# First mixer of a hybrid encoder: a third buffer for queries, keys and gates, all input projections ahead of the second group's values, and one output norm for two heads

## The chip, the cores and the metric

The kernel runs on one core of a Trainium2 chip. The metric is the device time of one execution in microseconds; a profiled execution also leaves a trace, whose span (first to last instruction) is a little shorter than the execution's time. Five engines work side by side: PE (TensorE, matmuls into PSUM), DVE (VectorE), ACT (ScalarE), POOL (GpSimd) and SP, which here only issues DMAs. Each takes its instructions in the order in which the program gives them and waits on semaphores for the others.

## The reference, cut to what matters

The model is four pre-norm residual layers (an even mixer, a feed-forward layer, an odd mixer, a feed-forward layer) over 512 positions of width 1024 in float32. The change is in the even mixer, the first layer:

```python
p = jnp.einsum('bsd,de->bse', h, w_in)
gq, gk, gv, gr, glf, glb, hq, hzf, hzb, hi, hg = _split(p, EVEN_COLS)
a = gla_mixer(gq, gk, gv, gr, glf, glb, wa2, ba, gla_g)          # 4 heads
bm = hgrn2_mixer(hq, hzf, hzb, hi, hg, lb_f, lb_b, hgrn_g)       # 4 heads
y = jnp.concatenate([a, bm], axis=-1)
return jnp.einsum('bse,ed->bsd', y, w_out)
...
# in both: o = bidir_scan(q, k_f, k_b, v, log_gates...); o = head_rmsnorm(o, norm_g); return o * silu(gate)
```

Each head has 64 key and 128 value channels. A gated linear attention runs over the positions in both directions; its output is normalised per head and position, multiplied by a gain and by a gate.

## The kernel before, in words

Heads go in pairs p = 0 to 3: pairs 0 and 1 are the first head group (GLA), pairs 2 and 3 the second (HGRN2). Heads are u = 2p and 2p + 1. A projection matmul multiplies a float32 weight chunk, split into a high and a low part (`h_`, `l_`, made by ACT and DVE in `load_split`), with the input, split likewise (`xh_m`, `xl_m`): 24 matmuls of 512 columns for each tile of 128 outputs.

For a pair the kernel makes queries `q`, keys `k` and gates `a` (tiles for both directions). Then `scores(p)` builds the attention scores: `products(0)`, the diagonal, and then seven levels h = 1, 2, 4, ... 64. At each level PE makes one set of small products in `sc` (two PSUM banks used in turns), DVE multiplies `q` and `k` by the running gate products, and a predicated copy takes the level's products from `sc` into `s`. The last level, 64, goes from `sc` into the score tile `A` on ACT. So PE and DVE take turns, and the next level's products wait for DVE. `attend(p)` follows: transposes of k (`kT`), states (`dS` on PE, `Si` on DVE), outputs `o` in PSUM, the norm of the outputs (Square on ACT, a sum on DVE, a power of -0.5 on POOL in `rstd`, a multiplication on DVE), transposes `oT`, and `finish(u)`, which multiplies with the gate `r` and splits the result into `yh` and `yl` for the output projection `wo`. For heads 4 to 7, `yh` and `yl` take over the buffers of the input tiles `xh_m`, `xl_m` (tag `xh`, `xl`, eight each). The tiles `o` have two buffers.

The order on PE is made when the program is written, by `Sched`. *Jobs* (projections `j_q`, `j_k`, `j_hq`, `j_hz`, values `j_v`, gates `j_gate`, output projection `j_out`) stand in one list and hand PE three matmuls at a time. *Chains* (`gates`, `scores`, `attend`) are put in between: each `yield W[...]` says after how much further matmul work, by an estimate in ns, the chain goes on. `self.sch.now` is that estimate's clock. A `yield` of a condition waits until another chain has got to a point. Nothing in this is decided on the chip; a chain that comes too early there makes PE wait.

The jobs' order before is values of group 0 (`v0`), gates g0 and g1, values of group 1 (`v1`), projections of pair 2 (`h2`: `p_hq2`, `p_hz0`, `p_hz1`), g2, g3, `h3`, g4 to g7, then `wo`. The tiles q, k and a have two buffers, so the projections of pair 2 wait until `attend(0)` has read those of pair 0.

Of the kernel before, what the change touches and what calls it, by code (L numbers as in the profile page):

```python
# [18 lines left out]
S = 512  # L19
# [5 lines left out]
S5PAD = 48  # L25

W = {
# [12 lines left out]
}  # L40

FAST = ("q1", "q2", "qk1", "qk2")
# [93 lines left out]
class Net:  # L136
# [261 lines left out]
    def even(self):  # L398
# [58 lines left out]

        def pair(p):
            if p not in P:
                P[p] = [pool.tile([128, w], F32, tag=n, name=f"{n}{p}", bufs=2)  # L460
                        for pool, n, w in ((ep, "q", S2), (ep, "k", KW), (em, "a", AW))]
            return P[p]

# [65 lines left out]
        def gates(p):  # L529
            af = pair(p)[2]  # L530
            a = dirs(af)
            yield W["z"]
            for d in range(2):
                i = 2 * p + d
                pz = hd_ps([128, S], f"z{i}")
                self.mm(pz, wa[:, i, :], lr)

                b = ba[:, i : i + 1]
                t = et([128, S], "e", f"e{i}", 2)
                nc.scalar.activation(t, pz, AF.Abs, bias=b)  # L540
                V.tensor_scalar(
                    out=a[:, d], in0=pz, scalar1=b, scalar2=0.0, op0=ALU.add, op1=ALU.min)
                nc.scalar.activation(t, t, AF.Exp, scale=-1.0)
                nc.scalar.activation(t, t, AF.Ln, bias=1.0)
                V.tensor_tensor(out=a[:, d], in0=a[:, d], in1=t, op=ALU.subtract)
            nc.scalar.activation(af[:, 0:S2], af[:, 0:S2], AF.Exp, scale=1.0 / 16.0)
            self.sch.chain(scores(p), W[f"sc{p}"])
# [35 lines left out]
            return x[:, :, 0:nb-1:2, :]  # L583

        def scores(p):
            yield (lambda: (p == 0 or p - 1 in scored) and (p < 2 or p - 2 in att)), 0.0
            q, k, a = P[p]
            t = em.tile([128, S + 8], F32, tag=f"t{p % 2}", name=f"t{p}", bufs=1)
            s = et([128, 2, 256], f"s{p % 2}", f"s{p}", 1)
            s4 = s.rearrange("p e (J c) -> p e J c", c=64)  # L590
            A = et([128, 2, 4, 128], "A", f"A{p}", 2)

            def products(h):

                half = 256 * (next(turn) % 2)
                ps = two[:, :, half : half + 256].rearrange("p e (J c) -> p e J c", c=64)
                for J in range(4):
                    for d in range(2):  # L600
                        for b in range(2):
                            for e in range(2):
                                r = slice(64 * e, 64 * e + 64)
                                o = S * d + 128 * J + 64 * b
                                out = ps[64 * b : 64 * b + 64, e, J, :]
                                st, w = k[r, o : o + 64], q[r, o : o + 64]
                                if h == 0:
                                    if d == 0:
                                        self.mm(out, k0[r, o : o + 64], w, cost=30)
                                elif h == 64:  # L610
                                    if b == d:
                                        o += 64 - 128 * d
                                        self.mm(out, st, q[r, o : o + 64], cost=60)
                                else:
                                    half = lambda v: v.rearrange(
                                        "p (n two h) -> p n two h", two=2, h=h)[:, :, 1 - d, :]
                                    self.mm(half(out), st, half(w), cost=25)
                return ps


            k0 = k
            if p >= 2:
                k0 = et([128, S], "e", f"ks{p}", 2)
                V.tensor_tensor(out=k0, in0=k[:, 0:S], in1=k[:, S:S2], op=ALU.add)
            psd = products(0)
            V.tensor_tensor(out=q, in0=q, in1=a[:, 0:S2], op=ALU.mult)
            T, h = a, 1
            while h <= 64:
                nb = S // h
                n = nb // 2  # L630
                if h == 1:
                    nc.scalar.activation(s, psd.rearrange("p e J c -> p e (J c)"), AF.Copy,
                                         scale=2.0 if p < 2 else 1.0)
                yield W[f"lv{p}_0"] if h == 1 else W[f"lv{p}"]
                ps = products(h)
                for x, half, tt in (
                        (right_left(q, nb, h), right_left, left_right(T, nb, 1)),
                        (left_right(k, nb, h), left_right, right_left(T, nb, 1))):
                    V.tensor_tensor(
                        out=x, in0=x, in1=tt.to_broadcast([128, 2, n, h]), op=ALU.mult)  # L640
                nT = (t if h in (1, 4, 16) else a) if h < 64 else self.stile([128, 8], "t128", f"t128_{p}", 2)
                t2 = T[:, 0 : 4 * n].rearrange("p (n two) -> p n two", two=2)
                V.tensor_tensor(out=nT[:, 0 : 2 * n], in0=t2[:, :, 0], in1=t2[:, :, 1], op=ALU.mult)
                l, r = slice(0, 64), slice(64, 128)
                if h <= 32:
                    i = LV.index(h)
                    V.copy_predicated(
                        out=s4, mask=masks[:, i : i + 1, :].unsqueeze(1).to_broadcast([128, 2, 4, 64]),
                        data=ps)
                else:  # L650
                    nc.scalar.activation(A[l, :, :, r], ps[l], AF.Copy)
                    nc.scalar.activation(A[r, :, :, l], ps[r], AF.Copy)
                if h == 32:
                    nc.scalar.activation(A[l, :, :, l], s4[l], AF.Copy)
                    nc.scalar.activation(A[r, :, :, r], s4[r], AF.Copy)
                T = nT
                h *= 2
            scored.add(p)
            AS[p] = (A, T)
            self.sch.chain(attend(p), W[f"at{p}"])  # L660
# [15 lines left out]
        def attend(p):  # L676
# [39 lines left out]
            for J in range(4):  # L716
                c = slice(128 * J, 128 * J + 128)
                ds = [d for d in range(2) if J != 3 * d]
                for d in ds:
                    for e in range(2):  # L720
                        self.mm(pss[e][:, J, :], Q[heads[e], d, c], Sis[d][heads[e], J, :],
                                False, J == 3)
            for e in range(2):
                u, ps = 2 * p + e, pss[e]
                sq = self.actp.tile([128, 4, 128], F32, tag="nsq", name=f"osq{u}", bufs=2)
                nc.scalar.activation(sq, ps, AF.Square)
                ss = self.stile([128, 4], "ss", f"ss{u}", 2)
                V.tensor_reduce(out=ss, in_=sq, axis=mybir.AxisListType.X, op=ALU.add)
                col = self.rstd(ss, 128, 4, f"o{u}")
                o = et([128, 4, 128], "o", f"o{u}", 2)  # L730
                V.tensor_tensor(
                    out=o, in0=ps, in1=col.unsqueeze(2).to_broadcast([128, 4, 128]), op=ALU.mult)
                rest.append((u, o))
            att.add(p)
            for u, o in rest:
                yield W[f"cs{p}"]
                pt = sm_ps(f"oT{u}")
# [70 lines left out]

        def jh(p):
            o = 4 + 3 * (p - 2)  # L810
            jw(j_hq, (p,), I["we_qk"][o], f"hq{p}", lambda: p - 2 in att)
            for d in range(2):
                jw(j_hz, (p, d), I["we_qk"][o + 1 + d], f"hz{p}{d}")

# [4 lines left out]
        self.sch.jobs[0]["got"] += first  # L819
        jw(j_q, (1,), I["we_qk"][2], "qk2")  # L820
        jw(j_k, (1,), I["we_qk"][3], "qk3")
        for o in "v0 g0 g1 v1 h2 g2 g3 h3 g4 g5 g6 g7".split():
            {"v": jv, "g": jg, "h": jh}[o[0]](int(o[1]))
        for ns in ((0, 1, 2, 3), (4,), (5,), (6,), (7,)):
            J(lambda *c, ns=ns: j_out(ns, 6 if len(ns) > 1 else KD, *c),
# [846 lines left out]
```

## Time and profile before

| | |
|---|---|
| three runs | 1271.01 to 1275.57 us, median 1273.41 us |
| the profiled execution | 1272.47 us, its span 1270.7 us |
| PE busy | 1242.3 us, 98% of the span |
| DVE, ACT, POOL busy | 66%, 39%, 15% |
| first mixer, on PE | from the start to about 262 us |

PE is nearly always busy, so its rest is the thing to look at: where it stands still, and where its matmuls are slow. In a row of the timeline the first number is the start, the second the length in us, and a bracket at the end gives the idle time ahead of the instruction and what ended it. PE's matmuls overlap, so two starts, not one length, tell what a matmul costs. The trace counts two matmuls for each float32 matmul of the program with small tiles (32 in place of 16 for one diagonal).

### The profile page before, as it was taken

To read this page: it belongs to the slowest core of one execution; us is meant where nothing else is said; L and a number is where in the kernel's file an instruction comes from. 1 tells how busy PE (TensorE), PEld (TensorE's weight loads), DVE (VectorE), ACT (ScalarE), POOL (GpSimd) and SP (SyncE) were. 2 spreads that over 40 slices of the span, in tenths; PEclk is the share of its full clock that TensorE was granted. 3 is DMA by queue.
4 is the path that set the end of the run, shared out by engine and by line. 5 is a ranking of instruction groups with operands and counts; after the bars stand their busy time and mean duration, and the time that the engine had idled before them with its cause. 6 is when DMAs were issued, how large, how long until landed. Compare 5 with 4: busy or idle time off the path is not lost.

```text
span 1270.7 us, 19272 instructions
## 1 busy us (share of the span) xinstructions
PE 1242.3 (98%) x7739; PEld 1030.1 (81%) x7739; DVE 834.8 (66%) x1320; ACT 490.4 (39%) x663; POOL 186.8 (15%) x280
## 2 busy tenths in 40 slices
PE   9999997999999999999999999999999999999997
PEld 7777876788888888878888889888888888888886
DVE  6576685567998487647666785776577537755753
ACT  6433442253434244334352334334344324423442
POOL 0000000032036607110031330002100000000012
PEclk9999998999999999999999999999999999999999
DMA  7131421233224333434257442332332333223211
GB/s 251 35 101 30 135 70 35 67 117 93 91 83 147 119 109 100 139 105 131 79 180 227 141 127 77 115 116 83 100 95 91 97 100 100 88 95 104 88 58 67
DMA packets 54202, 132.97 MB, mean 105 GB/s; under 512 B 12256, under 2 KB 17632, under 8 KB 54112
## 3 DMA queue, kind: packets, MB, share of 16 engines
q1 hardware_dynamic: 53392, 131.19, 32.7%
q8 instruction: 61, 1.00, 0.3%
q10 hardware_dynamic: 720, 0.55, 0.1%
q14 instruction: 29, 0.24, 0.1%
HBM read 120.17 MB, written 11.53 MB: 104 GB/s over the span
## 4 chain that ended last, share of the span: by engine, by line
PE 84%; DVE 10%; issue 2%; ACT 2%; POOL 1%; DMA 0%; POOLq 0%; SPq 0%; ACTq 0%; DVEq 0%
PE pu L191 31%; PE pd L191 17%; PE wo L191 6%; PE v L191 3%; PE p_g L191 3%; PE p_q L191 2%; PE sc L191 2%; PE p_k L191 2%; PE ov L191 2%; PE p_rg L191 2%; PE p_hz L191 2%; DVE c L312 2%; PE rv L191 2%; DVE l_u L183 1%; PE pl L191 1%
## 5 line engine op out<-in xcount | busy, mean ns | idle before, releaser
L191 PE MATMUL pu<-xh_f,h_u 128*128 128x512 f32 x704 | 275.6, 392 | 0.0
L191 PE MATMUL pu<-xh_f,l_u 128*128 128x512 f32 x704 | 274.1, 389 | 0.0
L191 PE MATMUL pu<-xl_f,h_u 128*128 128x512 f32 x704 | 274.0, 389 | 0.0
L191 PEld LDWEIGHTS pu<-xh_f,l_u 128*128 128x128 f32 x704 | 132.1, 188 | 27.6
L191 PEld LDWEIGHTS pu<-xh_f,h_u 128*128 128x128 f32 x704 | 132.2, 188 | 27.4
L191 PEld LDWEIGHTS pu<-xl_f,h_u 128*128 128x128 f32 x704 | 132.2, 188 | 27.0
L181 ACT ACTIVATE h_u<-r_u 128x1024 fp32r<-128x1024 f32 x88 | 93.2, 1059 | 129.1 <-PE pd L191 59.9
L312 DVE SCALAR_TENSOR_TENSOR c<-upad,convp,c 128x512 f32<-128x512 f32 x176 | 136.5, 777 | 3.8 <-ACT c L309 1.1
L191 PE MATMUL pd<-gh,h_d 128*128 128x512 f32 x331 | 129.3, 391 | 0.2 <-ACT gh L322 0.2
L191 PE MATMUL pd<-gl,h_d 128*128 128x512 f32 x331 | 128.9, 389 | 0.2 <-DVE gl L323 0.2
L191 PE MATMUL pd<-gh,l_d 128*128 128x512 f32 x331 | 128.9, 389 | 0.0
L183 DVE TENSOR_TENSOR l_u<-r_u,h_u 128x1024 fp32r<-128x1024 f32 x88 | 109.3, 1242 | 14.8 <-ACT h_u L181 14.1
L305 DVE TENSOR_TENSOR upad<-pu,rstd_f 128x512 f32<-128x512 f32 x88 | 60.6, 689 | 71.6 <-PE pu L191 69.8
L345 DVE TENSOR_TENSOR x<-pd,x 128x512 f32<-128x512 f32 x45 | 31.1, 691 | 102.8 <-PE pd L191 102.8
L309 ACT ACTIVATE c<-upad,convp 128x512 f32<-128x512 f32 x88 | 71.3, 812 | 23.0 <-DVE upad L305 19.9
L181 ACT ACTIVATE h_d<-r_d 128x896 fp32r<-128x896 f32 (+1 forms) x48 | 47.2, 988 | 70.8 <-PE pd L191 39.8
L191 PEld LDWEIGHTS pd<-gh,h_d 128*128 128x128 f32 x331 | 62.1, 188 | 13.4 <-ACT gh L322 0.6
L191 PEld LDWEIGHTS pd<-gl,h_d 128*128 128x128 f32 x331 | 62.2, 188 | 13.3 <-DVE gl L323 0.5
L322 ACT ACTIVATE gh<-g 128x512 fp32r<-128x512 f32 x44 | 27.8, 631 | 116.9 <-DVE g L319 116.9
L191 PEld LDWEIGHTS pd<-gh,l_d 128*128 128x128 f32 x331 | 62.1, 188 | 12.9
L317 ACT ACTIVATE sa<-c 128x512 f32<-128x512 f32 x44 | 27.8, 632 | 82.0 <-DVE c L312 82.0
L183 DVE TENSOR_TENSOR l_d<-r_d,h_d 128x896 fp32r<-128x896 f32 (+1 forms) x48 | 55.5, 1157 | 4.9 <-ACT h_d L181 2.6
(409 smaller groups left out, 2281.7 us busy)
## 6 DMA issues: line engine op xcount, KB each, us to landing
r_u<-in_w_up SPq DMA_DIRECT2D x88, 512.0 KB, 3.5
r_d<-in_w_down SPq DMA_DIRECT2D x32, 448.0 KB, 3.3
r_wo<-in_w_out SPq DMA_DIRECT2D x16, 512.0 KB, 3.5
r_d<-in_w_down SPq DMA_DIRECT2D x16, 512.0 KB, 3.5
w<-dw SPq DMA_DIRECT2D x20, 256.0 KB, 4.2
r_v<-in_we_v SPq DMA_DIRECT2D x8, 512.0 KB, 3.5
r_g<-in_we_g SPq DMA_DIRECT2D x8, 512.0 KB, 3.6
r_ov<-in_wo_v SPq DMA_DIRECT2D x8, 384.0 KB, 3.1
```

The source lines that it names most:

```text
L181: nc.scalar.activation(hi[:, 0:n], raw[:, 0:n], AF.Copy)
L183: eng.tensor_tensor(out=lo[:, 0:n], in0=raw[:, 0:n], in1=hi[:, 0:n].bitcast(F32), op=ALU.subtract)
L191: self.nc.tensor.matmul(ps, a, b, start=start, stop=stop)
L305: nc.vector.tensor_tensor(out=u[:, 1 : S + 1], in0=pss[half], in1=self.rbc, op=ALU.mult)
L309: nc.scalar.activation(c, u[:, 1 : S + 1], AF.Identity, scale=cw[:, 1:2], bias=cw[:, 3:4])
L312: nc.vector.scalar_tensor_tensor(out=c, in0=u[:, o : o + S], scalar=cw[:, tap : tap + 1], in1=c, op0=ALU.mult, op1=ALU.add)
L317: nc.scalar.activation(sa, cs[0], AF.Silu)
L322: nc.scalar.activation(h, g, AF.Copy)
L345: nc.vector.tensor_tensor(out=x[k], in0=ps, in1=x[k], op=ALU.add)
```

## The change

- `pair(p)`: q, k and a have three buffers in place of two; the projections of pair 2 wait for nothing now, those of pair 3 for `attend(0)`.
- The jobs' order puts `h2` and `h3` ahead of `v1`; the gates g2 to g7 come behind `v1`.
- `scores(p)`: the wait ahead of a pair's diagonal gets `W["next"]`, 3600 ns of estimated matmul work, for all pairs but the first; for pairs 2 and 3 the sum of the two directions' keys (`ks`) moves ahead of that wait.
- `gates(p)`: the two directions' small matmuls `z` stand 1200 ns apart.
- `attend(p)`: the norm of both heads has one tile of sums, one `rstd` of eight columns, then a `yield W["on..."]` of 5000 ns (3000 for pair 3), and only then the two multiplications. `att.add(p)` stands ahead of the norm.
- Nineteen numbers of `W` differ or are new, most of them for the estimated distance between levels and after `attend`.

```diff
-    "at0": 2500.0, "at1": 3645.0, "at2": 1800.0, "at3": 1600.0, "cs0": 5425.0, "cs1": 4500.0,
+    "at0": 2500.0, "at1": 3645.0, "at2": 1800.0, "at3": 1600.0, "cs0": 2500.0, "cs1": 2500.0,
...
+    "tr2": 7812.0, "tr3": 5000.0, "z": 1500.0, "z1": 1200.0, "next": 3600.0, 
+    "on0": 5000.0, "on1": 5000.0, "on2": 5000.0, "on3": 3000.0,
...
-                P[p] = [pool.tile([128, w], F32, tag=n, name=f"{n}{p}", bufs=2)
+                P[p] = [pool.tile([128, w], F32, tag=n, name=f"{n}{p}", bufs=3)
...
+                if d:
+                    yield W["z1"]
...
         def scores(p):
-            yield (lambda: (p == 0 or p - 1 in scored) and (p < 2 or p - 2 in att)), 0.0
             q, k, a = P[p]
+
+            k0 = k
+            if p >= 2:
+                k0 = et([128, S], "e", f"ks{p}", 2)
+                V.tensor_tensor(out=k0, in0=k[:, 0:S], in1=k[:, S:S2], op=ALU.add)
+            yield (lambda: (p == 0 or p - 1 in scored) and (p < 2 or p - 2 in att)
+                   ), W["next"] * (p > 0)
...
+            att.add(p)
+            ss = self.stile([128, 8], "ss", f"ss{p}", 2)
             for e in range(2):
-                u, ps = 2 * p + e, pss[e]
-                sq = self.actp.tile([128, 4, 128], F32, tag="nsq", name=f"osq{u}", bufs=2)
-                nc.scalar.activation(sq, ps, AF.Square)
-                ss = self.stile([128, 4], "ss", f"ss{u}", 2)
-                V.tensor_reduce(out=ss, in_=sq, axis=mybir.AxisListType.X, op=ALU.add)
-                col = self.rstd(ss, 128, 4, f"o{u}")
-                o = et([128, 4, 128], "o", f"o{u}", 2)
+                sq = self.actp.tile([128, 4, 128], F32, tag="nsq", name=f"osq{2 * p + e}", bufs=2)
+                nc.scalar.activation(sq, pss[e], AF.Square)
+                V.tensor_reduce(out=ss[:, 4 * e : 4 * e + 4], in_=sq, axis=mybir.AxisListType.X,
+                                op=ALU.add)
+            col = self.rstd(ss, 128, 8, f"o{p}")
+            yield W[f"on{p}"]
+            for e in range(2):
+                o = et([128, 4, 128], "o", f"o{2 * p + e}", 2)
                 V.tensor_tensor(
-                    out=o, in0=ps, in1=col.unsqueeze(2).to_broadcast([128, 4, 128]), op=ALU.mult)
-                rest.append((u, o))
-            att.add(p)
+                    out=o, in0=pss[e], op=ALU.mult,
+                    in1=col[:, 4 * e : 4 * e + 4].unsqueeze(2).to_broadcast([128, 4, 128]))
+                rest.append((2 * p + e, o))
...
-            jw(j_hq, (p,), I["we_qk"][o], f"hq{p}", lambda: p - 2 in att)
+            jw(j_hq, (p,), I["we_qk"][o], f"hq{p}", lambda: p < 3 or p - 3 in att)
...
-        for o in "v0 g0 g1 v1 h2 g2 g3 h3 g4 g5 g6 g7".split():
+        for o in "v0 g0 g1 h2 h3 v1 g2 g3 g4 g5 g6 g7".split():
```

What that makes of the order of instructions is shown at three places. The first is DVE's queue where the output norm of heads 0 and 1 meets the levels of pair 1's scores. Before, with `nvar` the input of POOL's power and `ncol` its result:

```order
L728 TENSOR_REDUCE ss0_1127<-osq0_1125 128x4
L728 TENSOR_REDUCE ss1_1137<-osq1_1135 128x4
L249 TENSOR_SCALAR nvar_o0_1129<-ss0_1127 128x4
L639 TENSOR_TENSOR q1_403<-q1_403,a1_405 128x2x64x4
L731 TENSOR_TENSOR o0_1133<-o0_1103,ncol_o0_1130 128x512
L249 TENSOR_SCALAR nvar_o1_1139<-ss1_1137 128x4
L639 TENSOR_TENSOR k1_404<-k1_404,a1_405 128x2x64x4
L731 TENSOR_TENSOR o1_1143<-o1_1104,ncol_o1_1140 128x512
L647 COPY_PREDICATED s1_925<-masks_124,sc_255 128x512
```

And now, same engine and place:

```order
L732 TENSOR_REDUCE ss0_1062<-osq0_1063 128x4
L732 TENSOR_REDUCE ss0_1062<-osq1_1066 128x4
L643 TENSOR_TENSOR q1_403<-q1_403,t1_942 128x2x128x2
L250 TENSOR_SCALAR nvar_o0_1069<-ss0_1062 128x8
L643 TENSOR_TENSOR k1_404<-k1_404,t1_942 128x2x128x2
L651 COPY_PREDICATED s1_943<-masks_124,sc_255 128x512
L647 TENSOR_TENSOR t1_942<-a1_405 128x128
L738 TENSOR_TENSOR o0_1163<-o0_1040,ncol_o0_1070 128x512
L738 TENSOR_TENSOR o1_1165<-o1_1041,ncol_o0_1070 128x512
```

The two multiplications that need POOL's result have moved behind the level's predicated copy. The second place is PE where pair 0's scores end (level 64 of `q0,k0`) and pair 1's begin (diagonal of `q1,k1`). Before:

```order
L191 MATMUL p_g1_886<-xh_m04_199,l_g1_473 128x512
L191 MATMUL sc_255<-q0_357,k0_358 64x64 x16
L191 MATMUL sc_255<-q1_403,k1_404 64x64 x16
L191 MATMUL p_g1_886<-xh_m05_206,h_g1_472 128x512
L191 MATMUL p_g1_886<-xl_m05_207,h_g1_472 128x512
```

Now twelve matmuls of `p_g1`, the transposes and three more of `p_g1` stand between the two; the last of them:

```order
L192 MATMUL p_g1_886<-xl_m05_207,h_g1_493 128x512
L192 MATMUL p_g1_886<-xh_m05_206,l_g1_494 128x512
L692 MATMUL kT00_927<-ident_72,k0_358 128x128 x3
L692 MATMUL kT01_933<-ident_72,k0_358 128x128 x3
L192 MATMUL p_g1_886<-xh_m06_215,h_g1_493 128x512
L192 MATMUL p_g1_886<-xl_m06_216,h_g1_493 128x512
L192 MATMUL p_g1_886<-xh_m06_215,l_g1_494 128x512
L192 MATMUL sc_255<-q1_403,k1_404 64x64 x16
L192 MATMUL dS00_963<-v0_0_581,kT00_931 64x128 x2
```

The pairs 1 and 2, and 2 and 3, are parted by eighteen projection matmuls in the same way. The third place is DVE's queue at the output norm of heads 6 and 7, ahead of the transposes `oT6`. Before:

```order
L728 TENSOR_REDUCE ss6_2691<-osq6_2689 128x4
L728 TENSOR_REDUCE ss7_2701<-osq7_2699 128x4
L249 TENSOR_SCALAR nvar_o6_2693<-ss6_2691 128x4
L249 TENSOR_SCALAR nvar_o7_2703<-ss7_2701 128x4
L731 TENSOR_TENSOR o6_2697<-o6_2667,ncol_o6_2694 128x512
L731 TENSOR_TENSOR o7_2707<-o7_2668,ncol_o7_2704 128x512
```

And now:

```order
L732 TENSOR_REDUCE ss3_2567<-osq7_2571 128x4
L250 TENSOR_SCALAR nvar_o3_2574<-ss3_2567 128x8
L759 TENSOR_TENSOR r6_2597<-p_g6_2513,rstd_m0_393 128x512
L184 TENSOR_TENSOR l_wo0_2_2603<-r_wo0_2_2600,h_wo0_2_2602 128x1024
L777 TENSOR_TENSOR yl4_2444<-o4_2411,yh4_2443 128x512
L777 TENSOR_TENSOR yl5_2504<-o5_2413,yh5_2503 128x512
L738 TENSOR_TENSOR o6_2593<-o6_2545,ncol_o3_2575 128x512
```

The multiplication of `o6` now stands behind a weight split (`l_wo0_2`) and behind `yl4` and `yl5`. On PE `oT6` stands twelve matmuls into the last gate projection `p_g7`.

## Rows read from the trace of the kernel before

**Rows 1.** PE's waits from 30 to 262 us: engine, line, releaser: total, times, longest.

```profile
PE sc L191 <- DVE s L647: 7.0, 2, 5.2
PE sc L191 <- ACT A L652: 4.8, 2, 3.4
PE kT L688 <- DVE k L639: 0.6, 1, 0.6
```

**Rows 2.** Timeline of PE, 81 to 221 us: start, length, instruction, idle before.

```profile
81.41 0.69 PE L191 MATMUL sc<-q,k 64*64 64x64 f32 x32 [1.47 <-ACT A L652]
...
102.96 1.14 PE L191 MATMUL sc<-q,k 64*64 64x32 f32 x64 [1.78 <-DVE s L647]
...
107.71 0.39 PE L191 MATMUL v<-l_v,xh_m 128*128 128x512 f32 x1
...
112.89 0.60 PE L739 MATMUL oT<-ident,o 128*128 128x128 f32 x4
113.25 0.48 PE L191 MATMUL v<-h_v,xh_m 128*128 128x512 f32 x1
...
114.82 1.13 PE L191 MATMUL sc<-q,k 64*64 64x32 f32 x64
115.88 0.50 PE L191 MATMUL v<-h_v,xh_m 128*128 128x512 f32 x1
116.22 0.39 PE L191 MATMUL v<-l_v,xh_m 128*128 128x512 f32 x1
116.45 0.40 PE L191 MATMUL v<-h_v,xl_m 128*128 128x512 f32 x1
...
193.00 1.13 PE L191 MATMUL sc<-q,ks 64*64 64x64 f32 x32 [3.37 <-ACT A L652]
...
196.64 0.39 PE L191 MATMUL p_g<-xh_m,h_g 128*128 128x512 f32 x1
...
215.35 1.93 PE L191 MATMUL sc<-q,k 64*64 64x32 f32 x64 [5.18 <-DVE s L647]
...
220.54 0.39 PE L191 MATMUL p_g<-xh_m,h_g 128*128 128x512 f32 x1
```

**Rows 3.** Windows: length, busy time by engine (instructions), PE's granted clock, DMA.

```profile
218.00:221.00 3.00, 3.00 (x11) 2.39 (x10) 2.02 (x5) 0.00 (x0) 0.00 (x0) 0.61 0.55 175
```

**Rows 4.** Timeline of DVE and of POOL, 96 to 103 us.

```profile
96.48 1.28 DVE L728 TENSOR_REDUCE ss<-osq 128x4 f32<-128x512 f32 x2 [2.69 <-ACT osq L726]
...
99.33 0.69 DVE L731 TENSOR_TENSOR o<-o,ncol_o 128x512 f32<-128x512 f32 x1 [0.91 <-POOL ncol_o L251]
...
100.00 0.69 DVE L639 TENSOR_TENSOR k<-k,a 128x512 f32<-128x512 f32 x1
101.59 0.69 DVE L731 TENSOR_TENSOR o<-o,ncol_o 128x512 f32<-128x512 f32 x1 [0.90 <-POOL ncol_o L251]
102.19 0.71 DVE L647 COPY_PREDICATED s<-masks,sc 128x512 f32<-128x512 int32 x1
...
100.17 1.38 POOL L251 TENSOR_TENSOR ncol_o<-nvar_o,mhalf 128x4 f32<-128x4 f32 x1 [0.88 <-DVE nvar_o L249]
```

**Rows 5.** Timeline of PE, ACT and DVE where `p_g7` starts, 226 to 230 us.

```profile
226.39 0.40 PE L191 MATMUL p_g<-xh_m,h_g 128*128 128x512 f32 x1
...
227.37 0.61 ACT L769 ACTIVATE yh<-o 128x512 fp32r<-128x512 f32 x1
...
228.41 0.61 ACT L769 ACTIVATE yh<-o 128x512 fp32r<-128x512 f32 x1
...
228.64 1.29 DVE L770 TENSOR_TENSOR yl<-o,yh 128x512 fp32r<-128x512 f32 x2
```

**Rows 6.** Groups of DVE's instructions, 30 to 260 us: count, busy us, mean ns.

```profile
L647 DVE COPY_PREDICATED s<-masks,sc 128x512 f32<-128x512 int32 x24 | 17.6, 734 | 0.0
...
L183 DVE TENSOR_TENSOR l_v<-r_v,h_v 128x1024 fp32r<-128x1024 f32 x6 | 7.3, 1217 | 0.8 <-ACT h_v L181 0.8
...
L568 DVE TENSOR_SCALAR a<-a,oml,lb 128x512 f32<-128x512 f32 x4 | 2.2, 544 | 1.3 <-ACT a L565 1.3
```

More of the change, by code (lines that the diff above doesn't have):

```diff
@@ L618, in products @@
                 return ps
[L621 to L624, printed above, removed]
             psd = products(0)
```

11 rows, old and new, of the table W are left out of this document.

## The prediction, on record before the changed kernel ran

> **What bounds the kernel now.** I read the page first: PE is busy for 98% of the span, so the change can win only where PE stands still or works slowly, and can lose only by giving PE new waits or more work. It adds no matmul and takes none away, and from the second half of the output projection to the end each engine's order is the same as before. All of it is decided in the first mixer, up to 262 us.
>
> There the view of waits gives PE three lasting releasers [rows 1]: the predicated copy of a level's products (7.0 us in two waits), the copies into the score tile `A` (4.8 us in two), and `k` ahead of a transpose (0.6 us). Together 12.4 us. The timeline places the four large ones [rows 2]: 1.47 us at 81.41, 1.78 at 102.96, 3.37 at 193.00, 5.18 at 215.35.
>
> A wait costs more than itself. Behind three of the four, projection matmuls start 0.43 us apart in place of 0.23; the granted clock in the window of 218 to 221 us is 0.61 [rows 3], so most of that stretch ran at the lower of the clock's two levels (1.2 of 2.4 GHz). To size it I use starts at full speed [rows 2]: a level's products 1.06 us (114.82 to 115.88), the transposes `oT` 0.36 (112.89 to 113.25), the first matmul behind small ones 0.34 (115.88 to 116.22), each further one 0.23 (116.22 to 116.45), a diagonal 0.69 at most (81.41).
> - 102.96 to 107.71: products, `oT`, first matmul, six more took 4.75 us; at full speed 1.06 + 0.36 + 0.34 + 6 x 0.23 = 3.14. Lost 1.6.
> - 193.00 to 196.64: diagonal, first, five more took 3.64; at full speed 0.69 + 0.34 + 5 x 0.23 = 2.18. Lost 1.5.
> - 215.35 to 220.54: products, `oT`, first, five more took 5.19; at full speed 2.91. Lost 2.3.
>
> Together 5.4 us. Behind the wait of 1.47 us at 81.41 there is no such stretch.
>
> **The change, part by part.**
>
> *Distance between a pair's last products and the next pair's diagonal.* The diagonal waits for ACT's copies of level 64, whatever half of `sc` it writes: before, the two sets stood back to back, and PE waited 1.47 and 3.37 us. Now 15 projection matmuls and the transposes stand between them for pair 1, 18 for pairs 2 and 3: 18 x 0.23 = 4.1 us. The longest such wait was 3.37, so it is covered. Gain: 4.8 us and the 1.5 us of slow matmuls.
>
> *The norm's two multiplications behind the predicated copy.* Before, DVE stood twice for POOL, 0.9 us each, and did two multiplications ahead of the copy for which PE waits [rows 4]. Now the copy is ahead. At pair 0 it needs, from the start of the sums: two sums 1.28, `q`, `k` 0.6 each, the copy 0.7 [rows 4], some 3.2 us; the sums begin about 0.7 us after the level's products begin (my estimate: the Squares come first), so the copy ends 3.9 us behind that, and the next products stand 1.06 + 18 x 0.23 = 5.2 us behind. The 7.0 us go, and 3.9 us of slow matmuls with them. POOL's power now has eight columns: between 1.38 us, as with four [rows 4], and twice that, 2.8. Either end lies beside the copy and eleven or more matmuls before `oT` asks for the result; I take no cost.
>
> *The third buffers and the jobs' order.* They let pair 2's projections run beside pair 1's levels and `v1` beside pair 2's. The weights that PE needs are the same, each used for 24 matmuls (5.5 us); a split of one chunk costs DVE 1.22 us [rows 6], so there is time for it per chunk. But evacuations, weight splits, the norm of heads 2 and 3 and the gates of pair 3 now fall on the same levels of pair 2. I add them up, from the sums of heads 2 and 3 to the copy of pair 2's level 8: sums 1.28, three levels of 0.6 + 0.6 + 0.64, two weight splits of 1.14, two evacuations and two norm multiplications of 0.6, and six small gate operations of about 0.4 (starts as in [rows 4], a little under the lengths of [rows 6]; the last figure and 0.6 for the short operations between levels are estimates): 1.28 + 5.5 + 2.3 + 2.4 + 2.4 + 0.6 = 14.5 us, beginning 0.7 us behind the level's start, so 15.2. PE has beside it three sets of products (3.2), 48 matmuls (11.0), two `oT` (0.7) and five returns to projections (0.1 each, 0.34 against 0.23): 15.4 us. That is almost even. If DVE is a tenth slower there, PE waits 1.3 us; at the other end nothing. I take 0.3, being nearer to even than to a tenth.
>
> *A new wait at `oT6`.* The `o` tiles have two buffers, so the product `o6` must wait for `yl4` to have read `o4`. `yh4` in its turn takes the buffer of `xh_m0`, which the last gate projection `p_g7` reads first. Before, that chain is in the trace with nobody waiting: `p_g7` starts at 226.39, `yh4` 0.98 us later, `yl5` ends at 229.93 [rows 5], 3.54 us behind `p_g7`'s start, and the same weight split lies between. Now DVE does `o6` behind `yl5`: 3.5 + 0.6 = 4.1 us. On PE `oT6` stands twelve matmuls into `p_g7`: 0.1 + 12 x 0.23 = 2.9 us. PE waits 1.3 us. Bounds: nothing, if PE reaches `p_g7` while ACT is already free, and 2.5 if a split more comes between; I take 1.3, the row's. It is of the size of the wait at 81.41, which left the clock alone.
>
> *More interruptions.* PE changes between projections and small matmuls eight times more (four there and back; `z` alone takes two). A return costs 0.11 us more than a matmul [rows 2]; with as much on the way in, 0.2, so 4 x 0.2 = 0.8 us. Bounds 0.4 and 1.
>
> *At nothing:* the earlier `ks`, hidden by 18 matmuls (0.6 us on DVE if not); the tile of eight sums; the DMAs of `wo` and the residual, moved past each other on SP's queue but issued 20 us ahead of use.
>
> **The sum**, against the profiled execution: 1272.47 - 12.4 - 5.4 + 1.3 + 0.3 + 0.8 = 1257.1 us. It lies 0.94 us under the median of the three runs, so 1258 us.
>
> **The rivals.**
> 1. *The new wait drops the clock*, as that of 1.78 us did and that of 1.47 did not [rows 2]. Price 1.6 to 2.3 us: 1260. For it: the sizes are close. Against: it lies among projections, as that at 81.41 did. [...]
> 2. *DVE becomes the bound of pair 2's levels.* Two or three of its levels wait 1 to 2 us, one or two with slow matmuls behind: 3 to 7 us more, 1261 to 1265. For it: the 15.2 against 15.4 above. Against: before, DVE was 66% busy on the whole. A rule would add to it: the Trainium skill ("SBUF — State Buffer", Who interferes with whom) says that POOL and DVE share a port pair which one instruction holds to its end. The row has a multiplication of 0.69 us beside a power of 1.38 us [rows 4], none of them visibly long. By the rule the copy behind `nvar` could wait up to 1.4 us in pair 2, giving 1259 to 1260; by the row nothing.
> 3. *The waits are moved, not removed.* The chain of levels is as long as before, and `A` or `s` may come late elsewhere: 1270 to 1276. Against: the order puts 4 us of projections ahead of each set of products.
> 4. *Slower.* The whole of pairs 1 and 2, twelve levels with projections, evacuations and splits beside them, becomes bound by DVE, each level waiting like that at 102.96: 1.78 + 1.6 = 3.4 us each. Six such levels, 20 us, eat the gain of 15; eight, 27 us, give 1258 + 27 = 1285. For it: every level then has a split or an evacuation more than before. Against: one level's own work is 1.9 us and a split and an evacuation 1.8, together under the 5.2 us of a level.
>
> **How the numbers follow.** First case with its own spread (1255 to 1260): 0.67. Rival 1: 0.11. Rival 2: 0.12. Rival 3: 0.06. Rival 4: 0.04. A measurement of this kernel can tell about 0.3% (4 us) from no change. Faster is the first case with rivals 1 and 2, 0.90; the same and slower are rivals 3 (mostly same) and 4: 0.05 and 0.05. The range goes from 1254 (all 17.8 us won without new costs, 1255.6, and the runs' scatter) to 1265, the end of rival 2.
>
> **What the changed profile would show.** PE's waits up to 247 us: none on `A`, none over 1.5 us on `s`, one of about 1.3 us on `o` ahead of `oT6`; the granted clock at 1.0 in every window from 30 to 240 us; the mixer about 15 us shorter and everything behind it as long as before. The prediction is wrong if sets of products in pair 2 wait for `s` by more than 1 us, if the clock falls behind `oT6`, or if PE's matmuls are slow where it did not wait.

## The result, and the profile after

The changed kernel took 1255.89 us (median of four runs, 1254.23 to 1257.63), the kernel before 1273.37 us beside it: ratio 0.9858, interval 0.9845 to 0.987. A second series gave 1257.57 us, ratio 0.9873, interval 0.9858 to 0.9888. The forecast was 1258 us, 1254 to 1265. The profiled execution took 1257.63 us, its span is 1255.8 us.

PE's waits from 30 to 270 us in the kernel after (engine, line, releaser: total, times, longest) are one row:

```profile
PE oT L746 <- DVE o L738: 1.3, 1, 1.3
```

The three releasers of [rows 1] are gone. The windows of the kernel after (length, busy time of PE, PEld, DVE, ACT and POOL, granted clock, DMA) have the clock at 1.00 from 30 to 240 us, here in two of four windows; before it was 0.61 in the window of 3 us of [rows 3] and 0.97 over the whole mixer:

```profile
80.00:125.00 45.00, 45.00 (x688) 36.69 (x687) 35.64 (x63) 21.31 (x32) 2.02 (x1) 1.00 0.21 67
...
180.00:240.00 60.00, 58.73 (x598) 48.74 (x598) 35.13 (x58) 21.17 (x31) 3.92 (x10) 1.00 0.22 71
```

The one wait is where [rows 5] had its cause. Timeline of the kernel after, 216 to 223 us, ACT, DVE, POOL and PE:

```profile
218.92 0.61 ACT L776 ACTIVATE yh<-o 128x512 fp32r<-128x512 f32 x1
...
218.18 0.69 DVE L759 TENSOR_TENSOR r<-p_g,rstd_m 128x512 f32<-128x512 f32 x1 [1.47 <-PE p_g L192]
219.05 1.23 DVE L184 TENSOR_TENSOR l_wo<-r_wo,h_wo 128x1024 fp32r<-128x1024 f32 x1 [0.17 <-ACT h_wo L182]
220.19 1.29 DVE L777 TENSOR_TENSOR yl<-o,yh 128x512 fp32r<-128x512 f32 x2
221.40 1.28 DVE L738 TENSOR_TENSOR o<-o,ncol_o 128x512 f32<-128x512 f32 x2
...
216.86 1.64 POOL L252 TENSOR_TENSOR ncol_o<-nvar_o,mhalf 128x8 f32<-128x8 f32 x1 [11.02 <-DVE nvar_o L250]
...
222.13 0.66 PE L746 MATMUL oT<-ident,o 128*128 128x128 f32 x4 [1.27 <-DVE o L738]
222.55 0.48 PE L192 MATMUL p_g<-xh_m,h_g 128*128 128x512 f32 x1
222.86 0.39 PE L192 MATMUL p_g<-xl_m,h_g 128*128 128x512 f32 x1
```

POOL's result is there at 218.50, but `o6` is queued behind the weight split and the two `yl`; PE goes on at full speed behind the wait (222.55 to 222.86).

The levels of pair 2, which [rows 4, 6] priced, are at the edge and no more. DVE and PE of the kernel after, from the sums of heads 2 and 3 on:

```profile
133.74 1.28 DVE L732 TENSOR_REDUCE ss<-osq 128x4 f32<-128x512 f32 x2 [2.62 <-ACT osq L731]
...
142.36 0.73 DVE L651 COPY_PREDICATED s<-masks,sc 128x512 f32<-128x512 int32 x1
...
147.24 0.73 DVE L651 COPY_PREDICATED s<-masks,sc 128x512 f32<-128x512 int32 x1
...
143.47 1.14 PE L192 MATMUL sc<-q,k 64*64 64x32 f32 x64
...
148.65 1.14 PE L192 MATMUL sc<-q,k 64*64 64x32 f32 x64
```

DVE has no idle time between the first of these rows and the third. The copy of level 4 ends (143.09) 0.38 us ahead of the products that wait for it, the copy of level 8 (147.97) 0.68 us.

Single executions of one kernel differ by 3 us and more, so times alone can't tell the parts apart. I take PE's stretch from the first `z` to the first `pu`, the first mixer without its input. Before and after, timeline of PE:

```profile
31.57 1.12 PE L191 MATMUL z<-lr,wa 64*128 64x512 f32 x2
...
286.10 0.39 PE L191 MATMUL pu<-xh_f,h_u 128*128 128x512 f32 x1
```

```profile
31.81 1.12 PE L192 MATMUL z<-lr,wa 64*128 64x512 f32 x2
...
269.36 0.39 PE L192 MATMUL pu<-xh_f,h_u 128*128 128x512 f32 x1
```

254.5 us before, 237.6 after: 17.0 us less. In the same way for all kernels below ("rest" is the mixer less PE's waits in it; ratio to the kernel before, with its interval):

| kernel | mixer us | waits us | rest us | median us, ratio |
|---|---|---|---|---|
| before | 254.5 | 12.6 | 241.9 | 1273.4 |
| before + norm | 246.4 | 7.2 | 239.1 | 1268.1, 0.9941 (0.9929 to 0.9954) |
| before + distance | 256.2 | 13.8 | 242.4 | 1277.0, 1.0016 (1.0007 to 1.0024) |
| before + buffers and order | 256.7 | 14.8 | 241.8 | 1278.4, 1.0035 (1.0022 to 1.0047) |
| before + norm + distance | 251.0 | 6.9 | 244.1 | 1266.7, 0.9937 (0.9924 to 0.9951) |
| before + gates not blocked | 249.5 | 10.1 | 239.4 | 1269.4, 0.9965 (0.9951 to 0.9978) |
| after | 237.6 | 1.3 | 236.3 | 1255.9, 0.9858 (0.9845 to 0.987) |
| after, once more | 237.6 | 1.3 | 236.3 | 1257.6, 0.9873 (0.9858 to 0.9888) |
| after, old buffers and order | 249.5 | 6.9 | 242.7 | 1269.0, 0.9954 (0.9941 to 0.9966) |
| after, distance 0 | 247.6 | 8.1 | 239.6 | 1266.1, 0.9944 (0.9928 to 0.996) |
| after, multiplications first | 242.0 | 5.4 | 236.6 | 1263.0, 0.9909 (0.9893 to 0.9925) |
| after + three DVE operations | 238.8 | 2.3 | 236.4 | 1258.8, 0.9888 (0.9871 to 0.9905) |
| after, longer wait at oT6 | 240.3 | 2.7 | 237.6 | 1259.5, 0.9891 (0.9877 to 0.9904) |
| after, three buffers of o | 236.1 | 0 | 236.1 | 1256.9, 0.9868 (0.9849 to 0.9887) |

The three parts alone change the mixer by -8.2, +1.7 and +2.1 us, -4.4 together; the whole change gives -17.0. The whole change has a fourth part: the longer distances between levels (`lv0` to `lv3` and their `_0`), with `sc0` and `z1`. It was never undone in the kernel after. "Before + norm + distance" and "after, old buffers and order" differ by it alone: 1.4 us of mixer (251.0 and 249.5), which their medians don't show. What it gives beside the new buffers and order stays open.

### The profile page after: what moved, and what is told of

Same layout as the page of the kernel before. It is cut to its first block, busy times and chain, and to the rows that moved or that the text cites. A ratio compares the mean times of both kernels' runs of the same rounds, so it can differ in the third digit from the quotient of the medians.

```text
span 1255.8 us, 19263 instructions
## 1 busy us (share of the span) xinstructions
PE 1237.9 (99%) x7739; PEld 1026.5 (82%) x7739; DVE 832.5 (66%) x1316; ACT 493.1 (39%) x665; POOL 185.3 (15%) x276
## 4 chain that ended last, share of the span: by engine, by line
PE 87%; DVE 10%; issue 2%; ACT 1%; POOL 1%; DMA 0%; SPq 0%; POOLq 0%; DVEq 0%; ACTq 0%
PE pu L192 31%; PE pd L192 18%; PE wo L192 6%; PE v L192 4%; PE p_g L192 3%; PE sc L192 2%; PE p_q L192 2%; PE p_k L192 2%; PE ov L192 2%; PE p_rg L192 2%; PE p_hz L192 2%; PE rv L192 2%; DVE c L313 2%; DVE l_u L184 1%; PE pl L192 1%
## 5 line engine op out<-in xcount | busy, mean ns | idle before, releaser
L310 ACT ACTIVATE c<-upad,convp 128x512 f32<-128x512 f32 x88 | 71.3, 812 | 22.6 <-DVE upad L306 19.4
```

Source lines behind the costliest of these rows:

```text
L310: nc.scalar.activation(c, u[:, 1 : S + 1], AF.Identity, scale=cw[:, 1:2], bias=cw[:, 3:4])
```

## The experiments

**The parts alone.** First the norm, put into the kernel before.

```diff
+            att.add(p)
+            ss = self.stile([128, 8], "ss", f"ss{p}", 2)
...
+            col = self.rstd(ss, 128, 8, f"o{p}")
+            yield W[f"on{p}"]
```

> The kernel before with the norm part alone (one norm for two heads, its multiplications 5000 ns of matmul work later, the oT distances of after). Theory of the prediction: the multiplications that wait for POOL stood ahead of the copy, so both waits on s go with their slow stretches, 10.9 us: about 1262.5 us. Rival: the wait of 5.18 us has a second cause. In the order of before only three projection matmuls stand between the two sets of products around it, because the gate projections there wait until a head is finished; so some 2 us of wait remain there, and a part of the slow stretch: only 1.78 + 1.6 + about 2.8 = 6.2 us go, about 1267 us, and the waits show one on s of about 2 us near 213 us.

The rival was right: 1268.1 us. Waits of this kernel, 30 to 270 us:

```profile
PE sc L191 <- ACT A L652: 4.8, 2, 3.4
PE sc L191 <- DVE s L647: 1.9, 1, 1.9
PE oT L742 <- DVE o L734: 0.5, 1, 0.5
```

The wait of 1.78 us of [rows 2] is gone, that of 5.18 has left 1.94, and 0.45 at the transposes behind it. So something else beside the norm's multiplications makes the second wait. In the kernel before, what stands ahead of that wait on PE is this (timeline):

```profile
208.14 1.14 PE L191 MATMUL sc<-q,k 64*64 64x32 f32 x64
209.21 0.50 PE L191 MATMUL p_g<-xh_m,h_g 128*128 128x512 f32 x1
209.54 0.40 PE L191 MATMUL p_g<-xl_m,h_g 128*128 128x512 f32 x1
209.78 0.40 PE L191 MATMUL p_g<-xh_m,l_g 128*128 128x512 f32 x1
```

Three matmuls, then the next set of products. `j_gate` of head u starts only when head u - 2 is finished; the jobs were stopped there, the chain's clock was set forward, and the level came early. This was tried by itself in the kernel before:

```diff
-                r = et([128, S], "r", f"r{u}", 2)
+                r = et([128, S], "r", f"r{u}", 4)
...
-            ... lambda: u < 2 or u - 2 in fin)
+            ... lambda: u < 4 or u - 4 in fin)
```

> The kernel before with four buffers for the gate tiles r and the gate projections waiting for the head four back in place of two; nothing else. Eighteen projection matmuls then stand between the two sets of products around the wait of 5.18 us, in place of three; the norm is as before. If the blocked gate projections are the larger cause of that wait: it falls by 15 x 0.23 = 3.4 us to about 1.7 us, the size of the wait at 102.96 (1.78), and the first mixer from z to pu takes about 251 us in place of 254.5. If the norm alone is the cause, as the prediction had it: 5 us as before.

The wait fell from 5.18 to 1.75 us (timeline of PE):

```profile
213.42 1.14 PE L191 MATMUL sc<-q,k 64*64 64x32 f32 x64 [1.75 <-DVE s L647]
```

So either step alone takes most of that wait away: the fifteen more matmuls 3.4 us, the norm 3.2 us (5.18 to 1.94; 2.8 if the 0.45 behind it is counted). Together that is more than the wait. The two causes overlap, and neither has a fixed share. Next the distance alone, and buffers and order alone.

```diff
+            yield (lambda: (p == 0 or p - 1 in scored) and (p < 2 or p - 2 in att)
+                   ), W["next"] * (p > 0)
```

> The kernel before with the distance of 3600 ns ahead of a pair's diagonal alone (and ks ahead of it). Theory of the prediction: both waits on A go, and 1.5 us of slow matmuls: 6.3 us, about 1267 us. Rival: with jobs in the order of before, the distance uses up projection matmuls that pair 3 then lacks; its states, diagonal, outputs and first two levels come one behind the other with no projection between, and PE waits there for kT, Si and s, about 2 us more than what the one wait on s of 5.18 us cost: about 1269 us.

1277.0 us: the rival's mechanism, with a price 8 us too low, about 6 if one allows for the kernel before, which took 1275.2 us beside it and 1273.4 in the first series. The waits on `A` ahead of the diagonals go, but those on `s` grow, and new ones come where the output projection stands for the last heads. Waits of this kernel:

```profile
PE sc L191 <- DVE s L648: 7.9, 2, 6.1
PE wo L191 <- ACT yh L770: 3.1, 2, 1.6
PE wo_sc L191 <- ACT A L653: 1.3, 1, 1.3
```

```diff
-                P[p] = [pool.tile([128, w], F32, tag=n, name=f"{n}{p}", bufs=2)
+                P[p] = [pool.tile([128, w], F32, tag=n, name=f"{n}{p}", bufs=3)
...
-        for o in "v0 g0 g1 v1 h2 g2 g3 h3 g4 g5 g6 g7".split():
+        for o in "v0 g0 g1 h2 h3 v1 g2 g3 g4 g5 g6 g7".split():
```

> The kernel before with three buffers, the condition and the jobs' order of after alone; norm and distances of before. If the parts only work together: the two waits on A stay (1.5 and about 3.4 us), the norms of pairs 0 and 1 each give a wait on s of about 1.8 to 2.5 us, and only the wait of 5.18 us, which came of three projection matmuls between two sets, goes: about 1270 us (1267 to 1273). If buffers and order are the larger part: about 1262 us.

1278.4 us: the parts only work together, and worse than I expected. The wait of 5.18 us went, but PE stood elsewhere, ahead of `dS`, of `oT` and on `ks`. Rows of its waits:

```profile
...
PE dS L191 <- DVE nvar_o L249: 3.2, 1, 3.2
...
PE oT L739 <- DVE o L731: 2.7, 1, 2.7
PE sc L191 <- DVE ks L624: 2.5, 1, 2.5
```

**Norm and distance without buffers and order**, once in the kernel before and once by undoing them in the kernel after (the last diff, reversed):

> The kernel before with both the norm part and the distance, but two buffers and the jobs' order of before. Theory that distances and norm do all of it, buffers and order nothing (the terms of the sum of the prediction): 17.2 us go, about 1256 us. Rival, that buffers and order give the room for the distances: where pair 2 ends and pair 3 begins no projection is left to stand between, PE waits there some 5 us (kT, Si, s, the norm) with about 2 us of slow matmuls: about 1263 us.

> The kernel after with two buffers, the condition and the jobs' order of before; all distances and the norm of after. If buffers and order give nothing by themselves: as after, about 1255 us, since the new wait of 1.3 us at oT6 goes too. If they give the room for the distances: PE waits some 5 us where pair 2 ends and pair 3 begins and is slow for about 2 us more, less the 1.3 us: about 1262 us, 1260 to 1267.

1266.7 and 1269.0 us: both keep less than half of the gain of 1.4%, and my price for what is lost was 4 to 7 us too low, 2 to 5 with the same allowance. The waits are 6.9 us in each. Timeline of PE in the kernel after with the old buffers and order; up to 206.51 no projection lies between the rows:

```profile
196.69 1.77 PE L192 MATMUL dS<-v,kT 128*64 128x128 f32 x24 [0.78 <-ACT kT L696]
198.40 0.69 PE L192 MATMUL sc<-q,ks 64*64 64x64 f32 x32
199.02 2.05 PE L192 MATMUL o<-v,A 128*128 128x128 f32 x16
201.00 1.61 PE L192 MATMUL o<-Si,q 64*128 64x128 f32 x24
202.54 1.13 PE L192 MATMUL sc<-q,k 64*64 64x32 f32 x64
206.51 1.93 PE L192 MATMUL sc<-q,k 64*64 64x32 f32 x64 [2.84 <-DVE s L651]
...
252.37 0.49 PE L192 MATMUL wo<-yh,h_wo 128*128 128x512 f32 x1 [1.51 <-ACT yh L776]
...
256.54 0.80 PE L192 MATMUL wo<-yh,h_wo 128*128 128x512 f32 x1 [1.50 <-ACT yh L776]
```

The gate projections are blocked again, two sets of products stand side by side, and pair 3 ends so late that `wo` waits for its `yh`, which I had not seen. Of the 12 us more than after, 5.6 are waits, and 6.4 lie in "rest" (242.7 against 236.3). By starts, some 4 us of these are slow matmuls behind the waits (my estimate): the set at 206.51 takes 1.93 us where that at 202.54 takes 1.13. The other 2 us are not traced.

**Undoing the other parts in the kernel after.** The distance:

```diff
-    ... "next": 3600.0, ...
+    ... "next": 0.0, ...
```

> The kernel after with the distance ahead of a pair's diagonal back at 0. By the prediction the waits on A return where two sets stand back to back, ahead of the diagonals of pairs 1 and 3: 1.5 us, and 1.5 to 3.4 us with up to 1.5 us of slow matmuls; 3 to 6 us in all: 1259 to 1262 us. Rival: the jobs' order had put enough between them, the distance gives nothing: 1256 us.

1266.1 us. The two waits on `A` came back as expected:

```profile
PE sc L192 <- ACT A L656: 3.9, 2, 2.5
```

A new wait of 1.70 us on `o` ahead of `kT`, and 2.04 in place of 1.27 at `oT`, I had not expected: the chain runs ahead of the heads before it. Behind the first wait on `A` (2.55 us) eleven projection matmuls were slow; of the 10.1 us of mixer 6.8 are waits and 3.3 "rest".

```diff
-            yield W[f"on{p}"]
             for e in range(2):
                 o = et([128, 4, 128], "o", f"o{2 * p + e}", 2)
...
+            yield W[f"on{p}"]
             for u, o in rest:
```

> The kernel after with the norm's two multiplications back ahead of the level's copy (the wait of 5000 ns behind them, PE's order unchanged). If the place of the two multiplications is what cost the 1.78 us at 102.96 before: DVE stands for POOL with the copy behind it, and the copies of three levels (pairs 0, 1 and 2) end some 1.4 us after PE is ready: three waits on s of about 1.35 us, 4 us in all, and 0 to 5 us of slow matmuls: about 1260 us, up to 1265. If the third buffers and the order alone removed these waits: as after, 1256 us, no wait on s over 0.3 us.

The three waits came at 1.35, 1.41 and 1.34 us (the third is put down to the short operation right behind the copy). DVE of this kernel at the first of them, and PE:

```profile
94.59 0.68 DVE L643 TENSOR_TENSOR k<-k,t 128x512 f32<-128x512 f32 x1
96.80 1.29 DVE L737 TENSOR_TENSOR o<-o,ncol_o 128x512 f32<-128x512 f32 x2 [1.53 <-POOL ncol_o L252]
98.01 0.72 DVE L651 COPY_PREDICATED s<-masks,sc 128x512 f32<-128x512 int32 x1
...
98.78 0.32 PE L192 MATMUL sc<-q,k 64*64 64x32 f32 x8 [1.35 <-DVE s L651]
```

DVE stands 1.53 us for POOL with the copy behind it. The profiled execution took 1259.1 us, the median is 1263.0.

**The edge in pair 2's levels, and the wait at `oT6`.** Three multiplications more on DVE, whose result nothing uses:

```diff
+                if p == 2 and h in (2, 4, 8):
+                    V.tensor_tensor(out=et([128, S], "dm", f"dm{h}", 1), in0=q[:, 0:S], in1=q[:, 0:S], op=ALU.mult)
```

> The kernel after with three more DVE multiplications of 128x512 (0.6 us each, their result is not used), one ahead of the copy in pair 2's levels 2, 4 and 8. The prediction had DVE almost even with PE there (15.2 against 15.4 us; the trace after has 0.38 us between the end of the copy of level 4 and the next products): two of the three come before the copy of level 4, so PE waits 0.9 us there and 0.4 us at the next, 1.3 us in all, and slow matmuls may follow: 1257 us, up to 1260. If DVE had room there, as its 66% on the page would say: no wait, 1256 us.

```profile
144.22 1.14 PE L192 MATMUL sc<-q,k 64*64 64x32 f32 x64 [0.79 <-DVE s L653]
149.69 1.02 PE L192 MATMUL sc<-q,k 64*64 64x32 f32 x56 [0.25 <-DVE s L653]
```

1.04 us in place of 1.3, at the two places named: there was less room than one such operation takes.

```diff
-                o = et([128, 4, 128], "o", f"o{2 * p + e}", 2)
+                o = et([128, 4, 128], "o", f"o{2 * p + e}", 3)
```

> The kernel after with three buffers for the tiles o in place of two, which puts the multiplication of o6 ahead of r6, the weight split and yl4, yl5 in DVE's queue. By the prediction's chain the wait of 1.27 us at oT6 goes and nothing else moves: about 1254.6 us. Rival: oT6 then waits for POOL's power instead, or the two splits behind are late for the output projection: 1256 us, with a wait elsewhere.

No wait is left on PE from 30 to 270 us, and the mixer is 1.4 us shorter than after (236.1). The time, 1256.9 us, does not show it: in its profiled execution `z` began 2.3 us later (34.09), behind a wait for the input. I count it as no slower than after, not as shown faster.

```diff
+                for i in range(2 * (p == 3 and e == 0)):
+                    V.tensor_scalar(out=o, in0=o, scalar1=1.0, scalar2=None, op0=ALU.mult)
```

(In DVE's queue `o7` and both of these stand ahead of what `oT6` waits for.)

> The kernel after with DVE's multiplication of o7 and two multiplications by 1 (about 0.4 us each) ahead of what oT6 waits for, so that PE's wait there is about 2.7 us in place of 1.27. Nothing else moves. If a wait among projections leaves the clock alone: 1.45 us more, about 1257.5 us, and projection matmuls 0.23 us apart behind it. If a wait of that length drops the clock wherever it lies, as the waits of 2.5 to 6 us ahead of sets of products did: five to eight matmuls 0.43 us apart behind it, 1.1 to 2.3 us more, about 1259 us.

```profile
223.45 1.11 PE L748 MATMUL oT<-ident,o 128*128 128x128 f32 x4 [2.66 <-DVE o L742]
...
224.79 0.63 PE L192 MATMUL p_g<-xl_m,h_g 128*128 128x512 f32 x1
225.21 0.63 PE L192 MATMUL p_g<-xh_m,l_g 128*128 128x512 f32 x1
```

So a wait among projections can drop the clock: behind this one of 2.66 us four matmuls were slow, and "rest" was 1.3 us longer. It need not: in "before + buffers and order" a wait of 2.72 us stands at an `oT` among matmuls of `p_g` too (242.04), and the next ones follow 0.23 us apart.

**The second mixer.** In the first profile after, the stretch from the first `rv` to the first `p_rg` was 24.0 us, before 22.7.

> The kernel after, once more. Its first profile had 1.4 us more than that of before between the second mixer's first rv and its first p_rg, at a lower granted clock. If that is the clock of one execution: the stretch is again 21 to 24 us long, and the first mixer, from z to pu, again 237.6 us within 0.3, with one wait of 1.27 us. If the change itself caused it: 24.0 us again. Time 1255 to 1257 us.

22.6 us this time, and the mixer 237.6 again: it was the clock of one execution. The other profiles say the same: the stretch took 21.0, 22.6 to 22.7 or 23.8 to 24.3 us, whatever the order (23.9 in "before + norm"). The windows from 700 to 710 us of the two profiles, first and second:

```profile
700.00:710.00 10.00, 7.35 (x40) 7.05 (x39) 5.47 (x9) 0.00 (x0) 1.04 (x1) 0.70 0.61 201
```

```profile
700.00:710.00 10.00, 7.36 (x46) 7.00 (x45) 5.86 (x9) 0.00 (x0) 1.43 (x1) 0.83 0.61 201
```

## Why the prediction was right, and where it was not

- **The time and the profile.** Everything that the changed profile was to show is there: no wait on `A` or `s`, one of 1.27 us (1.3 forecast) at `oT6`, no low clock up to 240 us, and a shorter mixer. Rivals 1 to 4 did not come.
- **Distance.** The reason holds: without it the waits on `A` return. It is worth more than the term (10.1 us of mixer against 6.3), since without it the chain also runs into heads that are not done.
- **"The norm's two multiplications behind the predicated copy ... The 7.0 us go, and 3.9 us of slow matmuls with them"** is the step that failed. It credits the norm with 10.9 us; put in alone it took 8.2 us off the mixer, and undone in the kernel after it cost 4.4. The wait of 1.78 us had the norm as its cause. That of 5.18 had two: the multiplications ahead of the copy, and only three matmuls between two levels, since the gate projections were blocked. The norm alone left 1.94 + 0.45 us there, unblocked gates alone 1.75. PE's timeline of before at that place would have told it: I priced the releaser of the wait and did not ask why the waiting set of products stood so near.
- **"The third buffers and the jobs' order"** had no gain of their own in the sum. Undone, they cost 12.0 us of 17.0. I read it so: they keep the gate projections behind work that finishes heads, and so give the matmuls that the distances use up. The timeline above, with no projection between two sets, and the kernel with unblocked gates fit that; unblocked gates with the old order and all the rest of the change, which would test it by itself, were not run. The sum came out because it counted every wait of before as gone, whichever part removes it.
- **Slow matmuls.** 5.4 us were counted and 0.8 us given back for interruptions, 4.6 net; "rest" fell by 5.7 (241.94 to 236.28). How much of the 1.1 us is fewer slow matmuls and how much cheaper interruptions stays open.
- **DVE in pair 2's levels.** 15.2 against 15.4 us was the forecast for the copy of level 8, 0.2 us of room; 0.68 us were there. The tightest place was level 4's copy, with 0.38. The three operations used both up. The 0.3 us for it did not come.
- **The sum.** The mixer was to win 15.4 us and won 17.0. The profiled span shows 14.9 of it, as 0.24 us came at the start, 1.4 in the second mixer by the clock, and the rest, 0.5, behind the last layer. That the profiled time (1257.63 us) lies 0.5 us from the forecast sum (1257.1) is luck in part: 1.6 us too little gain in the sum, and 2.1 us lost where it had nothing.
- **The port rule of rival 2.** No copy was late: DVE's multiplication beside the power kept its length (0.68 us). The power did not. In the fourteen first mixers a power of eight columns took 1.94 to 2.02 us each time that DVE had begun a multiplication `k` 0.16 to 0.24 us ahead of it, and 1.64 us (as at 216.86) each time that it had not. One of four columns took 1.31 to 1.39 us behind such a multiplication and 1.0 without, so the 1.38 us of [rows 4] already held some 0.35 us of it. In the kernel after:

```profile
135.61 0.68 DVE L643 TENSOR_TENSOR k<-k,t 128x512 f32<-128x512 f32 x1
...
135.78 2.01 POOL L252 TENSOR_TENSOR ncol_o<-nvar_o,mhalf 128x8 f32<-128x8 f32 x1 [38.97 <-DVE nvar_o L250]
```

  The Trainium skill ("SBUF — State Buffer", Who interferes with whom) has VectorE and GpSimd share a port pair that one instruction holds to its end. The trace agrees: DVE came first each time, and POOL, for which PE did not wait in the kernel after, was 0.3 to 0.4 us longer.

## What to carry to other kernels

Ask two things of every wait: what released it, and why the waiting work stood where it did; the second answer may lie in a scheduler that had nothing else to issue. Distances between steps need work to fill them, so a longer distance without a new order of jobs can cost more than it brings. Parts of such a change are not additive: undo each one in the finished kernel as well as putting each into the old one, and compare a stretch of the trace where whole times scatter.

## What the runs showed of the hardware that was not expected

The fall of the clock behind a wait is not settled by the wait's length alone. In the first mixers of these fourteen profiles, of fourteen waits of 1.27 to 1.47 us none was followed by slow projection matmuls; of nine of 1.70 to 2.04 us four were; of twelve of 2.5 us or more eleven were. The same wait of 1.78 us, at pair 0's norm, was followed by matmuls 0.43 us apart before (102.96, [rows 2]) and not in the kernel with the distance alone:

```profile
100.82 1.14 PE L191 MATMUL sc<-q,k 64*64 64x32 f32 x64 [1.78 <-DVE s L648]
...
102.61 0.39 PE L191 MATMUL v<-l_v,xh_m 128*128 128x512 f32 x1
102.84 0.39 PE L191 MATMUL v<-h_v,xl_m 128*128 128x512 f32 x1
```

Two waits of about 1.5 us some 3 to 4 us apart, ahead of `wo`, cost 9 to 15 slow matmuls in all three kernels that had them; one such wait of 1.50 us, in "before + gates not blocked", cost none. The Trainium skill ("TensorE: Matmul & The Clock Gate", What's actually happening) has the low level as the default, which activity releases; the trace agrees for eleven of the twelve waits of 2.5 us or more, and the rule by itself does not tell the two executions of 1.78 us apart.

A part of the scatter of times lies at the start. In single executions of "after", "after, three buffers of o" and "after, old buffers and order" PE's longest wait for its first input, at 6 to 8 us, was 0.55, 1.57 and 1.95 us; the granted clock from 8 to 16 us was then 1.00, 0.79 and 0.60, and `z` began at 31.81, 34.09 and 35.49 us.
